# The order of the steps beside the gather slots of a PEER layer, and how many steps stand in each slot

## The chip, the cores and the metric

The kernel runs on one core of a Trainium2 chip. The metric is the device time of one execution in microseconds; before the change three runs gave 883.9, 884.2 and 888.28 us, median 884.2 us. The core has a matrix engine (PE, with its weight loads PEld), a vector engine (DVE), a scalar engine (ACT), a general engine (POOL), which here also issues the gathers, and SyncE (SP), which issues the loads of weights. Each engine runs its instructions in the order in which the program wrote them, so an instruction that waits holds up everything behind it on the same engine. Sixteen DMA engines move the data.

## What is computed

One decoder layer over 256 positions of width 1024, in float32. Two groups of attention heads (MoBA, which is plain causal attention at this length, and differential attention) share one input projection; their output goes through `w_out` and is added to `x`. Then comes PEER, a retrieval of single-neuron experts:

```python
x = x + mixed @ w_out
q  = (xc @ w_query).reshape(C, 8, 2, 128)          # xc: the normed x, 128 tokens a chunk
sc = einsum('thpd,hpnd->thpn', q, sub_keys)
top_s, top_i = top_k(sc, 16)                       # of each half, then of the 256 sums
best_s, best_pos = top_k(cand_s, 16)
u, vv = expert_down[experts], expert_up[experts]   # 8 heads x 16 experts a token
act = gelu(einsum('cd,chkd->chk', xc, u))
out = einsum('chk,chkd->cd', softmax(best_s) * act, vv)
```

Each of the 256 tokens needs 128 experts, and each expert is a row of 2048 floats (down and up side by side): 268.85 MB of gathered rows.

## The kernel before

The tokens are two tiles of 128: A (the first half) and B (the second). A tile goes through six projections (`proj`, then `evac` with norm and RoPE, and `turn` for the transposes), attention by group (`scores`, `probsT`, `attend`, `mixturn`, together `both`), the output product (`wout`), the residual and its transposes (`resid`), the norm (`norm`), and then four **routings**: `route(tt, c4)` computes the queries of two heads (`query`) and picks their experts (`choose`: `keys`, `route1`, `route2`), which makes 32 more of the tile's 128 columns of expert numbers known (`ready` counts them).

A **slot** is one column of experts for the 128 tokens of a tile, 256 slots in all, A's 128 first. Its gather (L604, issued by POOL) brings 128 rows of 8 KB, 1.05 MB, into a buffer of a ring. `dot` (L614, DVE) multiplies the down half with the normed token and sums; `weigh` (L620 to L626, ACT) makes gelu, the gate and a diagonal matrix; `add` multiplies the up half with that diagonal on PE into `acc` (L638), or, in every fourth slot of A, adds it on DVE (L636). In the program's order `add` of a slot comes one slot behind its `dot`, and once `lag` is 1 `weigh` comes a slot later as well. After `add` the buffer is free and `issue()` writes the next gather, as long as expert numbers are known.

The ring starts with 4 buffers (`RING0`). Five more (`RING1`) come when the space of the projections' weights and work tiles is given back, and six more (`RING2`) when the attention's space is.

All of A up to its first half routing, and B's projections 5, 4 and 2, are written ahead of the slots. The rest is cut into **steps** by Python generators and written between the slots, in an order that is fixed by hand (`tc.manual_schedule()`), so the order of each engine's instructions is just the order of this program:

- `front()` is B up to its norm: projections 3, 0 and 1 (15 + 13 + 15 = 43 steps); in the 44th step the ring grows from 4 to 9 and `lag` becomes 1; attention of the two groups (16 steps each); `wout` with its loads (2 loads and 16 pairs of k and n: 18 steps; `wo2` holds 4 tiles of weights, half of what is needed, so the second half of the load waits for the first half of the products); `resid` 3, `norm` 2. Together 98 steps; after the last the ring has 15.
- `route(A, c4)` and `route(B, c4)`: 20 steps each, 8 of `query` and 12 of `choose`. After `query` the next routing's weights are loaded (`load_q`).
- `mix(r, f, nr, nf)` takes nf steps of f after every nr steps of r. `behind()` puts them in their order, and the loop at the end (L744 to L749) writes a slot, then steps until there are `STEPS` = 2 for each slot so far, then the gathers that are possible.

Before the change the order is: the other half of the first routing (12 steps), then route(A, 1) with one step of front after every two (30 steps), route(A, 2) and route(A, 3) with one after every one (40 each), the 48 steps left of front, and then B's four routings.

Weights of B's projections come through 8 tiles (`wts`), four to a projection, so that the load of the second next projection waits for the one whose tiles it takes over; each waits on SP, in the order of the program.

Of the kernel before, what the change touches and what calls it, by code (L numbers as in the profile page):

```python
# [45 lines left out]
RING1 = 5  # L46
RING2 = 6
WRING = 8
STEPS = 2.0

DVE_ADD = 4

# [2 lines left out]
def hymba_peer_kernel(ctx, tc, xT_d, x_d, an_d, fn_d, fnT_d, win_d, qkg_d, lam_d, og_d, wout_d,  # L55
# [324 lines left out]
    A, B = 0, 1  # L380
# [84 lines left out]
    def load_q(c4, pool):  # L465
        W["q", c4] = []
        fetch(("q", c4), wq_d[c4], pool)

    def query(tt, c4, parts=((0, 4),)):
        w = W["q", c4]  # L470
        q = rt1.tile([P, 4, P], FT, name="qs", tag="qs")
        qs[tt, c4] = q
        for a, b in parts:
            p = ps().rearrange("p (a b) -> p a b", b=P)
            for c in range(a, b):
                for k in range(KC):
                    PE.matmul(p[:, c], lhsT=w[k // 2][:, k % 2, c * P:(c + 1) * P], rhs=xgT[tt][:, k],  # L477
                              start=(k == 0), stop=(k == KC - 1))
                    if k % 4 == 3 and (c, k) != (b - 1, KC - 1):
                        yield  # L480
            S.copy(q[:, a:b], p[:, a:b])
            yield

    def keys(tt, c4, a, b):
        sc = scp.tile([P, 4, NKEY], FT, name="sc")[:, :b - a]
        p = ps().rearrange("p (a b) -> p a b", b=NKEY)[:, :b - a]
        for c in range(a, b):
            PE.matmul(p[:, c - a], lhsT=qs[tt, c4][:, c], rhs=sk[:, c4 * 4 + c], start=True, stop=True)
        S.activation(sc, p, AF.Copy, scale=r2[tt])  # L489
        scs[tt, c4, a] = sc  # L490
        yield
# [73 lines left out]
    def route2(tt, c4, h0, nh):  # L565
        hits, g = rs1.pop((tt, c4, h0))
        c0 = (c4 * 2 + h0) * TOPK
        fv = ef[tt][:, c0:c0 + nh * TOPK].rearrange("p (h k) -> p h k", h=nh)
        for i, e in enumerate(hits):
            V.tensor_reduce(fv[:, :, 8 * i:8 * i + 8], e, axis=AX.X, op=OP.add)  # L570
        V.tensor_copy(eid[tt][:, c0:c0 + nh * TOPK], ef[tt][:, c0:c0 + nh * TOPK])
        gz = small.tile([P, 2], FT, name="gz")[:, :nh]
        V.tensor_reduce(gz, g, axis=AX.X, op=OP.add)
        V.reciprocal(gz, gz)
        V.tensor_tensor(g, g, bc(gz, TOPK), op=OP.mult)

    def choose(tt, c4, h0=0, nh=2):
        yield from keys(tt, c4, 2 * h0, 2 * h0 + 2 * nh)
        yield from route1(tt, c4, h0, nh)
        yield  # L580
        route2(tt, c4, h0, nh)
        ready[0] += nh * TOPK

    def route(tt, c4, then=None):
        yield from query(tt, c4)
        if then is not None:
            load_q(then, wqp)
        yield from choose(tt, c4)
# [3 lines left out]
    rows, made, ready, done = {}, [0], [0], [0]  # L592
# [4 lines left out]
    def issue():  # L597
        while made[0] < ready[0] and rings:
            n = made[0]
            made[0] += 1  # L600
            tt, k = n // NSEL, cols[n]
            home[n] = rings.pop(0)
            rows[n] = home[n].tile([P, 2 * D], FT, name="uv")
            G.indirect_dma_start(out=rows[n], out_offset=None, in_=uv_d,  # L604
                                 in_offset=bass.IndirectOffsetOnAxis(ap=eid[tt][:, k:k + 1], axis=0))

    acc, lag, dots, ready_w = {}, [0], [], []
# [40 lines left out]
    def slots(n):  # L648
        for _ in range(n):
            dot()  # L650
            last = done[0] == NT * NSEL
            while len(dots) > (0 if last else lag[0]):
                weigh()
            while len(ready_w) > (0 if last else 1):
                add()
# [31 lines left out]
    def front():  # L687

        for g in (3, 0, 1):
            yield from project(g)  # L690
        pj.close()
        wst.close()
        bs = ExitStack()
        bp["b"] = bs.enter_context(tc.tile_pool(name="bp", bufs=1, side="right"))
        xb = ctx.enter_context(tc.tile_pool(name="xb", bufs=1))
        rings.extend([ctx.enter_context(tc.tile_pool(name="gat1", bufs=RING1))] * RING1)
        lag[0] = 1
        yield from both(B, MOBA)
        yield from both(B, DIFF)
        bs.close()  # L700
        wo2 = right.enter_context(tc.tile_pool(name="wo2", bufs=4, side="right"))
        for q in (0, 2):
            for n in range(2):
                fetch(("o", n, B), wout_d[n], wo2, (q, q + 1))
            yield
            for k in range(2 * q, 2 * q + 4):
                for n in range(2):
                    wout(B, n, k, psB)
                    yield
        yield from resid(B, xb)  # L710
        yield from norm(B, xb)
        right.close()
        rings.extend([ctx.enter_context(tc.tile_pool(name="gat2", bufs=RING2, side="right"))] * RING2)

    def mix(r, f, nr, nf):
        n = 0
        for _ in r:
            yield
            n += 1
            if n % nr == 0:  # L720
                for _ in range(nf):
                    next(f, None)
                    yield

    def behind():
        f = front()
        yield from choose(A, 0, 1, 1)
        yield from mix(route(A, 1, 2), f, 2, 1)
        yield from mix(route(A, 2, 3), f, 1, 1)
        yield from mix(route(A, 3), f, 1, 1)  # L730
        for _ in f:
            yield
        yield from route(B, 3, 2)
        yield from route(B, 2, 1)
        yield from route(B, 1, 0)
        yield from route(B, 0)

    ctx.enter_context(tc.manual_schedule())
    issue()
    work = behind()  # L740
    for _ in range(1):
        next(work)
    steps = 0
    while done[0] < NT * NSEL:  # L744
        slots(1)
        while steps < STEPS * (done[0] + 1):
            next(work, None)
            steps += 1
        issue()  # L749


# [54 lines left out]
```

## Time and profile before

| | |
|---|---|
| runs | 883.9, 884.2, 888.28 us; median 884.2 us |
| the profiled execution | 884.77 us, span 883.0 us from its first to its last instruction |
| moved by DMA in the span | 318.95 MB, 361 GB/s on average |
| of it gathers | 268.85 MB |
| first gather issued, first dot | at 103.7 us, at 112.8 us |
| PE, DVE, POOL, ACT busy | 688.5, 542.2, 411.7, 303.1 us |

The span is cut below at dots: a row with a line's name counts the two instructions of each dot (the product and the read of its sum), so 28 instructions are 14 slots. "PEclk" is the share of the full clock that PE was granted, "DMA share" the mean busy share of the DMA engines, GB/s what they moved. Times are in microseconds from the start of the span.

### The profile page before, as it was taken

What the parts mean: (1) busy time and instruction counts of PE and PEld (TensorE: products, weight loads), DVE (VectorE), ACT (ScalarE), POOL (GpSimd) and SP (SyncE); (2) the same over time, 40 slices, a digit from 0 to 9 for tenths busy, and PEclk for the clock granted to TensorE, in tenths of its full rate; (3) what the DMA queues carried; (4) which work ended last, traced back from release to release, by engine and by line L of the source; (5) the groups of instructions that cost most, each with busy time, mean ns of one, the idle gap of its engine ahead of it and who ended that gap; (6) DMA issues with size and microseconds to landing.
All of it is one profiled execution on the core that took longest, in us unless ns stands there. A gap on an engine that the chain in (4) does not pass through costs nothing.

```text
span 883.0 us, 8001 instructions
## 1 busy us (share of the span) xinstructions
PE 688.5 (78%) x2028; PEld 321.6 (36%) x2028; DVE 542.2 (61%) x1417; ACT 303.1 (34%) x909; POOL 411.7 (47%) x438
## 2 busy tenths in 40 slices
PE   6999959668559686867968769699888777877786
PEld 2555525234225243433625435244222222222222
DVE  4753485684694986671777876994455445554453
ACT  1322143133232363631233332454333333333332
POOL 3310363354362582232564764775555555455540
PEclk9999989899879877978989799799999999999999
DMA  9991779989969889789899999899999999999995
GB/s 352 348 371 42 275 273 341 419 317 351 416 239 321 301 355 403 245 311 379 332 416 418 420 417 419 311 409 419 419 420 419 421 420 419 420 420 421 419 419 212
DMA packets 51534, 318.95 MB, mean 361 GB/s; under 512 B 6112, under 2 KB 6368, under 8 KB 18592
## 3 DMA queue, kind: packets, MB, share of 16 engines
q0 software_dynamic: 36944, 268.85, 76.4%
q1 hardware_dynamic: 14112, 48.93, 14.5%
q10 hardware_dynamic: 432, 0.66, 0.2%
q8 instruction: 17, 0.28, 0.1%
q14 instruction: 29, 0.24, 0.1%
HBM read 317.36 MB, written 1.05 MB: 361 GB/s over the span
## 4 chain that ended last, share of the span: by engine, by line
DMA 44%; PE 25%; DVE 14%; issue 8%; POOL 5%; ACT 3%; POOLq 0%; DVEq 0%; SPq 0%; ACTq 0%
DMA uv<-in_uv_dram,eid 41%; PE acc L638 8%; PE psB L184 6%; DVE uv L614 5%; PE psA L477 3%; PE psB L352 3%; POOL uv L604 3%; DVE x L636 1%; POOL hit L556 1%; DMA w<-in_win_dram 1%; DMA w<-in_wq_dram 1%; DMA w<-in_wout_dram 1%; PE psA L254 1%; PE psA L303 1%; ACT L620 1%
## 5 line engine op out<-in xcount | busy, mean ns | idle before, releaser
L638 PE MATMUL acc<-uv,dg 128*128 128x512 f32 x896 | 464.6, 649 | 151.2 <-ACT dg L626 149.8
L604 POOL DMA_INDIRECT uv<-in_uv_dram,eid x256 | 319.2, 1247 | 352.0 <-PE acc L638 138.2
L614 DVE SCALAR_TENSOR_TENSOR uv<-uv,xn 128x1024 f32<-128x1024 f32 x256 | 314.0, 1237 | 216.7 <-DMA uv<-in_uv_dram,eid 213.4
L638 PEld LDWEIGHTS acc<-uv,dg 128*128 128x128 f32 x896 | 164.1, 200 | 407.8 <-ACT dg L626 269.4
L620 ACT ACTIVATE hdot<-hdot 128x1 f32<-128x1 f32 x256 | 51.3, 200 | 351.1 <-DVE uv L614 350.8
L626 ACT ACTIVATE dg<-ident,hdot 128x128 f32<-128x128 f32 x224 | 89.9, 401 | 42.4 <-PE acc L638 35.8
L184 PE MATMUL psB<-w,xT 128*128 128x512 f32 x192 | 94.9, 631 | 7.2 <-DMA w<-in_win_dram 7.2
L621 ACT ACTIVATE hdot<-hdot,gate 128x1 f32<-128x1 f32 x256 | 75.3, 294 | 8.3
L477 PEld LDWEIGHTS psA<-xgT,w 128*128 128x128 f32 x512 | 65.0, 197 | 19.0 <-issue 18.7
L477 PE MATMUL psA<-xgT,w 128*128 128x128 f32 x512 | 64.7, 279 | 0.0
L184 PEld LDWEIGHTS psB<-w,xT 128*128 128x128 f32 x192 | 37.5, 203 | 50.4 <-issue 48.5
L498 POOL TENSOR_TENSOR ci<-tf 128x4 f32<-128x4 f32 (+5 forms) x81 | 20.9, 291 | 58.8 <-DVE tf L526 58.8
L636 DVE SCALAR_TENSOR_TENSOR x<-uv,hdot,x 128x1024 f32<-128x1024 f32 x32 | 43.7, 1364 | 0.0
L352 PE MATMUL psB<-w,mT 128*128 128x512 f32 x64 | 30.9, 616 | 5.9 <-DMA w<-in_wout_dram 5.9
L556 POOL TENSOR_TENSOR hit<-hit,ci 128x160 f32<-128x160 f32 (+1 forms) x32 | 30.0, 968 | 0.5 <-DVE hit L553 0.4
L214 POOL TENSOR_TENSOR qt<-pr,rS 128x128 f32<-128x128 f32 (+1 forms) x24 | 18.2, 784 | 23.8 <-ACT pr L195 23.8
L510 DVE MAX8 tops<-sc 128x8 f32<-128x128 f32 x32 | 7.1, 280 | 23.4 <-ACT sc L489 23.4
L614 DVE DVE_READ_ACCUMULATOR uv<-uv,xn 128x1 f32 x256 | 20.8, 81 | 0.0
L352 PEld LDWEIGHTS psB<-w,mT 128*128 128x128 f32 x64 | 12.3, 198 | 20.8 <-issue 13.2
L570 DVE TENSOR_REDUCE ef<-hit 128x16 f32<-128x320 f32 (+3 forms) x18 | 11.8, 665 | 9.7 <-POOL hit L556 9.7
L360 DVE TENSOR_TENSOR x<-psB,x 128x512 f32<-128x512 f32 x4 | 2.8, 691 | 24.1 <-PE psB L352 24.1
L620 ACT ACT_TABLE_LOAD x13 | 16.7, 1283 | 0.2
(126 smaller groups left out, 417.7 us busy)
## 6 DMA issues: line engine op xcount, KB each, us to landing
w<-in_win_dram SPq DMA_DIRECT2D x40, 512.0 KB, 8.4
w<-in_wq_dram SPq DMA_DIRECT2D x28, 512.0 KB, 8.6
w<-in_wout_dram SPq DMA_DIRECT2D x16, 512.0 KB, 9.9
uv<-in_uv_dram,eid POOLq DMA_INDIRECT x256
sk<-in_sk_dram SPq DMA_DIRECT2D x1, 1024.0 KB
out_dram<-x SPq DMA_DIRECT2D x4, 256.0 KB, 2.0
xT<-in_xT_dram SPq DMA_DIRECT2D x2, 256.0 KB
x<-in_x_dram ACTq DMA_DIRECT2D x1, 512.0 KB
```

The source lines that it names most:

```text
L184: PE.matmul(p, lhsT=xT[tt][:, k], rhs=W[ci, tt][k // 2][:, k % 2], start=(k == 0), stop=(k == KC - 1))
L352: PE.matmul(wops[tt, n], lhsT=mixT[tt, MOBA if k < 4 else DIFF][:, k % 4], rhs=W["o", n, tt][k // 2][:, k % 2], start=(k == 0), stop=(k == ...
L477: PE.matmul(p[:, c], lhsT=w[k // 2][:, k % 2, c * P:(c + 1) * P], rhs=xgT[tt][:, k], start=(k == 0), stop=(k == KC - 1))
L498: eng.tensor_tensor(d, src[:, :, 1, b0:b0 + nb], src[:, :, 0, a0:a0 + 1].to_broadcast([P, src.shape[1], nb]), op=OP.add)
L556: G.tensor_tensor(e[:, h], e[:, h], ci[:, h, None, :n].to_broadcast([P, 8, n]), op=OP.mult)
L604: G.indirect_dma_start(out=rows[n], out_offset=None, in_=uv_d, in_offset=bass.IndirectOffsetOnAxis(ap=eid[tt][:, k:k + 1], axis=0))
L614: V.scalar_tensor_tensor(uv[:, :D], uv[:, :D], 1.0, xn[n // NSEL], op0=OP.mult, op1=OP.mult, accum_out=h)
L620: S.activation(h, h, AF.Gelu)
L621: S.activation(h, h, AF.Copy, scale=gate[n // NSEL][:, col:col + 1])
L626: S.activation(dg, ident, AF.Copy, scale=h)
L636: V.scalar_tensor_tensor(x2[tt], uv[:, D:], dg, x2[tt], op0=OP.mult, op1=OP.add)
L638: PE.matmul(acc[tt][:, c], lhsT=dg, rhs=uv[:, D + c * 512:D + (c + 1) * 512], start=(k == 0), stop=(k == NSEL - 1))
```

## The change

`STEPS` becomes a table of four rates, and `behind()` sets which of them holds. The half routing that is left is mixed with three steps of front to each of its own, and front then goes on alone until `lag` is set, that is until the projections are done and the ring has nine buffers. All that at four steps a slot. Then route(A, 1) alone at three a slot, route(A, 2) and route(A, 3) with one step of front after each of theirs and then the rest of front at two a slot, and B's routings at 1.2 a slot. The instructions themselves, their number and their data stay as they are.

```diff
-STEPS = 2.0
+STEPS = (4, 3, 2, 1.2)
...
+    rate = [0]
+
     def behind():
         f = front()
-        yield from choose(A, 0, 1, 1)
-        yield from mix(route(A, 1, 2), f, 2, 1)
+        yield from mix(choose(A, 0, 1, 1), f, 1, 3)
+        while not lag[0]:
+            next(f)
+            yield
+        rate[0] = 1
+        yield from route(A, 1, 2)
+        rate[0] = 2
         yield from mix(route(A, 2, 3), f, 1, 1)
         yield from mix(route(A, 3), f, 1, 1)
         for _ in f:
             yield
+        rate[0] = 3
         yield from route(B, 3, 2)
...
-    for _ in range(1):
-        next(work)
+    next(work)
     steps = 0
     while done[0] < NT * NSEL:
         slots(1)
-        while steps < STEPS * (done[0] + 1):
+        steps += STEPS[rate[0]]
+        while steps >= 1:
             next(work, None)
-            steps += 1
+            steps -= 1
         issue()
```

## The prediction

> **What bounds the kernel now.** I read the page's slices first: the span, how busy the DMA engines are, and what they move.
>
> ```profile
> span 883.0 us, 8001 instructions
> ...
> DMA  9991779989969889789899999899999999999995
> GB/s 352 348 371 42 275 273 341 419 317 351 416 239 321 301 355 403 245 311 379 332 416 418 420 417 419 311 409 419 419 420 419 421 420 419 420 420 421 419 419 212
> ```
>
> Forty slices of 22.1 us. From slice 20 on, the core moves some 420 GB/s: there nothing but the DMA engines decides, and one slice from the end shows it in full, beside the one dip:
>
> ```profile
> 551.90:573.90 22.00, 13.17 (x22) 4.93 (x22) 21.27 (x65) 9.07 (x25) 16.10 (x24) 0.77 0.85 311
> 838.90:860.90 22.00, 17.75 (x36) 6.09 (x36) 11.10 (x18) 7.68 (x27) 9.61 (x7) 1.00 1.01 420
> ```
>
> A slot's gather is 1.05 MB, so at 420 GB/s it takes 2.50 us, and no order of steps makes that half faster. What can be won lies before, where the rate falls to 239 or 245. I therefore cut the span where the program changes, at dots 0, 14, 53, 61 and 85 and at the end of B's routing.
>
> ```profile
> core 0: us, PE busy (x) PEld busy (x) DVE busy (x) ACT busy (x) POOL busy (x), PEclk, DMA share, GB/s
> 112.80:164.90 52.10, 36.41 (x124) 19.25 (x125) 35.19 (x114) 16.94 (x46) 23.34 (x30) 0.87 0.84 324
> 164.90:307.20 142.30, 99.32 (x313) 49.69 (x311) 101.01 (x279) 44.21 (x127) 65.68 (x84) 0.90 0.89 330
> 307.20:333.50 26.30, 21.95 (x74) 11.11 (x73) 21.90 (x64) 18.34 (x45) 21.51 (x29) 0.81 0.93 367
> 333.50:399.60 66.10, 46.38 (x167) 25.47 (x168) 44.26 (x97) 27.58 (x81) 16.88 (x16) 0.82 0.84 318
> 399.60:433.90 34.30, 28.41 (x97) 14.88 (x96) 12.70 (x28) 5.25 (x17) 11.26 (x10) 0.90 0.91 349
> 433.90:573.20 139.30, 101.25 (x379) 56.62 (x379) 111.50 (x375) 50.08 (x141) 88.46 (x111) 0.88 0.99 399
> 573.20:883.00 309.80, 249.80 (x518) 89.44 (x516) 159.34 (x261) 113.33 (x384) 158.70 (x116) 1.00 0.98 404
> ```
>
> The same stretches for the dots alone give the number of slots (two instructions a dot):
>
> ```profile
> core 0: us, DVE busy (x), PEclk, DMA share, GB/s
> 112.80:164.90 52.10, 17.59 (x28) 0.87 0.84 324
> 164.90:307.20 142.30, 50.46 (x79) 0.90 0.89 330
> 307.20:333.50 26.30, 9.65 (x15) 0.81 0.93 367
> 333.50:399.60 66.10, 22.74 (x41) 0.82 0.84 318
> 399.60:433.90 34.30, 6.06 (x11) 0.90 0.91 349
> ```
>
> So slots 0 to 13 took 52.1 us (3.72 each), 14 to 52 142.3 us (39 slots, 3.65), 53 to 60 26.3 us (8, 3.29), the next 20.5 took 66.1 (3.22), the last 5.5 of this part 34.3 (6.2). In no stretch before 433.9 is any engine full: PE is at 70% (36.41 of 52.1, 99.32 of 142.3), DVE at 68 and 71%, DMA at 0.84 to 0.89. The work is a ring of waits: a buffer is filled, read, added and only then filled again. With four buffers that ring sets the pace. The fifth comes at 316 us; POOL's timeline shows the gathers no longer waiting for an add:
>
> ```profile
> 309.51 0.94 POOL L604 DMA_INDIRECT uv<-in_uv_dram,eid  x1 [1.47 <-PE acc L638]
> ...
> 316.18 0.94 POOL L604 DMA_INDIRECT uv<-in_uv_dram,eid  x1 [0.30 <-issue]
> ...
> 322.39 1.45 POOL L604 DMA_INDIRECT uv<-in_uv_dram,eid  x1 [0.30 <-issue]
> ```
>
> **The order, counted in steps.** Before: 12 steps of the half routing, 30 of the first mix (10 of them front's), 40 of the second (20 of front's), then front's 44th step stands 28 steps into the third. That is step 110, slot 54 at two a slot. The third mix ends at step 122, front 48 steps later at 170, slot 84; B's routings at 250, slot 124. After: 12 + 36 mixed and 8 more steps of front bring its 44th at step 56, slot 14. Route(A, 1) needs 20 at three: slot 21. Two mixes of 40 at two: slot 61, with 84 of front's steps done. The last 14: slot 68. B's 80 at 1.2: slot 135. Expert numbers suffice throughout: 16 until slot 12, where the ring of four wants 16; 32 until slot 21, where nine buffers want 30; 64 to slot 41. The full ring of 15 comes at slot 68 in place of 84.
>
> **Stage 1, slots 0 to 13, four buffers, four steps.** The costs:
>
> ```profile
> L184 PE MATMUL psB<-w,xT 128*128 128x512 f32 x192 | 94.9, 631 | 7.2 <-DMA w<-in_win_dram 7.2
> ...
> L477 PE MATMUL psA<-xgT,w 128*128 128x128 f32 x512 | 64.7, 279 | 0.0
> ```
>
> A projection's products take 94.9/12 = 7.9 us, a query's 64.7/8 = 8.1. An add takes PE 64.63/29 = 2.2 us a slot (four instructions; a quarter of A's slots have none):
>
> ```profile
> 164.90:307.20 142.30, 64.63 (x116) 22.11 (x116) 0.90 0.89 330
> 307.20:333.50 26.30, 13.11 (x21) 4.45 (x21) 0.81 0.93 367
> 333.50:399.60 66.10, 25.75 (x45) 9.14 (x46) 0.82 0.84 318
> ```
>
> PE has 3 x 7.9 = 23.7 us of projections (8 steps of 0.99 us, three to a slot, ahead of the older slot's add) and 14 x 0.75 x 2.2 = 23: 47 us. DMA has 14 gathers and three projections' weights, 14.7 + 6.3 = 21 MB, 50 us at 420. At this ring's shares, 70% and 0.87, that is 67 and 57 us. I take 64, 4.6 a slot against 3.7 now. The bounds are 50 (DMA full) and 82 (PE's 47 and the 35 of DVE in these slots one after the other): the evacuations' chains (ACT, DVE, POOL, DVE, PE) come closer together, and POOL's part of them stands ahead of the gathers. SP's order changes too: three projections' loads now stand ahead of `load_q`, and they may be late:
>
> ```profile
> w<-in_wq_dram SPq DMA_DIRECT2D x20, 512.0 KB, 12.9
> w<-in_win_dram SPq DMA_DIRECT2D x9, 512.0 KB, 27.6
> ```
>
> The last projection's load starts when the third one's products are done, some 21 steps of front (seven slots, 32 us) before its own products; the median landing of 27.6 us fits in, barely. The next query's load has four slots, some 16 us, for 12.9. These waits stand in the 82.
>
> **Stage 2, slots 14 to 20.** In the stretch of B's routings DVE is busy 111.50 us, of which the dots and adds have these:
>
> ```profile
> L638 PE MATMUL acc<-uv,dg 128*128 128x512 f32 x127 | 72.9, 708 | 35.3 <-ACT dg L626 35.3
> ...
> L614 DVE SCALAR_TENSOR_TENSOR uv<-uv,xn 128x1024 f32<-128x1024 f32 x44 | 53.4, 1238 | 0.1
> ...
> L636 DVE SCALAR_TENSOR_TENSOR x<-uv,hdot,x 128x1024 f32<-128x1024 f32 x11 | 15.5, 1407 | 0.0
> ```
>
> 111.5 - 53.4 - 15.5 - 3.5 (reads of the sums, 44 x 0.08) leaves 39 us for four routings, 9.8 each. Seven slots need 7 x 1.66 + 9.8 = 21 us of DVE; at that stretch's 80% that is 27 us (bounds 21 and 34; the gathers for five more buffers go out here).
>
> **Stage 3, slots 21 to 60: nine buffers, one routing and one attention step a slot.** Slots 53 to 60 of before are just this mix: 3.29 us. The next stretch has two attention steps a slot and no routing: 3.22. By work: attention has 21.95 + 46.38 - 13.11 - 25.75 = 29 us of PE in these two stretches, 7 of it output products; with 40 x 0.75 x 2.2 = 66 of adds and two queries, 16, PE has 111 us; at 83% (21.95 of 26.3) 134, 3.35 a slot. DMA has 42 MB of gathers and 8.4 of weights, 120 us. I take 3.45, 138 us, a little over the rows, as queries (8.1 us each) and attention meet on PE. Bounds 120 and 167 (4.18, the mean from 333.5 to 433.9).
>
> **Stage 4, slots 61 to 67.** The same 14 steps took 34.3 us, and 11 of them were a wait for the second half of `w_out`:
>
> ```profile
> 399.64 10.97 DMA w<-in_wout_dram
> ```
> and from the timeline of DVE:
> ```profile
> 421.30 0.69 DVE L360 TENSOR_TENSOR x<-psB,x 128x512 f32<-128x512 f32 x1 [15.98 <-PE psB L352]
> ```
>
> DVE waited 16 us at that place, with the dots behind it. Now the first half's products stand one to a slot, beside a routing, and the load of the second half starts as each tile comes free; only the last tiles, freed just ahead, can be late. I take 8 of the 11 us off: 26 us; bounds 23 and 34.
>
> **The rest.** From dot 85 (433.9) to the end are 449.1 us. From dot 68 there are 17 gathers more, 42.5 us. The 1.2 steps keep DVE at 1.66 + 1.2 x 9.8/20 = 2.25 us a slot, below 2.50, where two steps gave 2.64; of the dip of 22 x (1 - 311/420) = 5.7 us I take off 3. No new wait is added; tail and B's slots stay.
>
> **The sum:** 112.8 + 64 + 27 + 138 + 26 = 367.8 for dot 68 (slot 84 at 433 before), and 367.8 + 449.1 + 42.5 - 3 = 856.4 us of span. The profiled execution lies 1.8 us over its span (884.77 against 883.0), 0.6 over the median of 884.2: **858 us**.
>
> A rule of the Trainium skill speaks against any gain: DMA: Bandwidth & Descriptors, Where 436 GB/s comes from, has transfers from HBM bound at about 358 GB/s a core. By it the 361 GB/s of the whole span are the limit already, and the sum would stay at 884. The trace disagrees: 420 GB/s in the slice quoted above.
>
> The other rule is for the change. TensorE: Matmul & The Clock Gate, Part 1, says that PE is slowed to half its clock once it has been idle for a window of some 3.4 us. The rows show 0.87 granted in the first stretch and 1.00 in the last one; if denser products kept the clock at 1.00, 47 us of PE would be 41, and the sum an estimated 6 us less. I leave this out.
>
> **The rivals.**
> - *The DMA engines are full from slot 21 on.* Nine buffers are enough and stage 3 takes its 120 us: 858 - 18 = 840. For it speaks 0.93 of DMA share from 307.2 to 333.5; against it 0.84 in the next stretch with the same buffers.
> - *The steps' time is only moved.* Buffers weren't the limit, the steps' chains were, and they cost what they did: 321.1 us from dot 0 to dot 85, less 17 slots at 2.5 us, puts dot 68 at 391.4, 23.6 later than the sum: 882. For it speaks that nine buffers gave 3.22 to 4.18 a slot, hardly below four buffers' 3.65.
> - *Adds come late on PE, and it is slower.* With nine buffers POOL still waited for PE's adds:
>
> ```profile
> POOL uv L604 <- PE acc L638: 56.3, 15, 9.4
> ```
>
>  In stage 3 an add stands behind a query's products and attention's transposes, and those wait for DVE. If every slot pays this, at 4.18 us, stage 3 is 167 us (+29) and stage 4 stays at 34 (+8): 895. It decides from 4.2 us a slot on alone: (888.6 - 858)/40 = 0.77 over 3.45. Against it speak the 3.29 of the very mix.
> - *The whole span's 361 GB/s is what the core can draw, whatever the order:* then DMA is the bound everywhere and the time stays at 884. Twenty slices at some 420 speak against it. This is the first of the two rules above.
>
> **Chances.** Forecast 0.58, full DMA 0.14, moved time 0.15, late adds 0.12, capped rate 0.01. A difference of 0.5%, 4.4 us, is about what a measurement tells from none: faster is below 879.8, slower above 888.6. So faster 0.72, same 0.16, slower 0.12. The forecast's own case runs from 840 (stage 1 at 57, stage 3 at 127) to 876 (stage 1 at 74, stage 3 at 146). The range takes in the moved time and stops short of the late adds: 840 to 890.
>
> **What would show it.** POOL's burst of five gathers stands near 177 us instead of 316; dot 21 near 204, dot 61 near 342, dot 68 near 368 (+-15). DMA is over 0.93 from dot 14 on and full from dot 68; the dip near 560 is gone. The wait for `w_out` shrinks from 11 us to a few. Wrong would be: stage 1 over 82 us with POOL waiting for adds or PE for weights, stage 3 over 4 us a slot, or a DMA rate below 400 after dot 68.

## The result and the profile after

The changed kernel took 848.25, 848.48 and 852.76 us, median 848.48 us against 884.2 us: a ratio of 0.960, 95% interval 0.954 to 0.966. Measured once more, beside the experiments below, it had 0.963 (0.960 to 0.966). The forecast was 858 us, with a range from 840 to 890.

These are the span, the DMA engines' share and their rate in the forty slices of the changed kernel; a slice is 21.2 us now. Lines of the code are one higher than before (L605 is the gather, L615 the dot, L639 the add on PE).

```profile
span 846.5 us, 8001 instructions
...
DMA  9992798669899999999999999999999999999993
GB/s 350 352 356 91 244 409 332 230 263 406 302 395 376 369 409 382 420 417 419 420 418 420 417 419 420 421 420 420 420 418 421 420 421 418 420 421 420 420 419 155
```

The full rate of 420 GB/s begins at slice 16, 339 us, in place of slice 20, 442 us, and it has no dip after that before the last slice. The lowest slices that are left are 3 and 4, ahead of the first dot (111.7 us), and 7 and 8, in stage 1 and at its end.

The same cut as in the prediction, at dots 0, 14, 21, 61 and 68 of the changed kernel (columns as before):

```profile
core 0: us, PE busy (x) PEld busy (x) DVE busy (x) ACT busy (x) POOL busy (x), PEclk, DMA share, GB/s
111.70:177.50 65.80, 45.17 (x98) 18.99 (x96) 49.57 (x135) 20.22 (x52) 31.93 (x43) 0.88 0.77 295
177.50:214.60 37.10, 28.31 (x123) 19.91 (x124) 22.08 (x87) 10.12 (x26) 21.49 (x28) 0.78 0.92 369
214.60:333.30 118.70, 103.44 (x416) 60.02 (x414) 99.59 (x290) 59.17 (x169) 62.87 (x72) 0.92 0.97 374
333.30:356.80 23.50, 21.33 (x69) 11.31 (x70) 16.00 (x33) 6.53 (x21) 8.06 (x8) 0.93 1.01 420
356.80:846.50 489.70, 376.25 (x958) 158.27 (x956) 291.43 (x672) 176.12 (x569) 259.70 (x245) 0.96 0.99 408
```

| stage of the changed kernel | forecast, us | measured, us | short of 420 GB/s, us |
|---|---|---|---|
| start to dot 0 | 112.8 | 111.7 | |
| 1: slots 0 to 13 | 64 | 65.8 | 65.8 x (1 - 295/420) = 19.6 |
| 2: slots 14 to 20 | 27 | 37.1 | 4.5 |
| 3: slots 21 to 60 | 138 | 118.7 | 13.0 |
| 4: slots 61 to 67 | 26 | 23.5 | 0 |
| the rest | 488.6 | 489.7 | 14.0 |

The last column says where the time came from: it is the time in which the bytes that were not moved would have been moved. Both kernels move the same bytes (318.95 and 318.93 MB), so this sum has to come out; it shows in which stretch the time was won, and the cause has to come from the runs below. The same sum over the seven stretches of the kernel before, from its rows in the prediction, is 11.9 + 30.5 + 3.3 + 16.1 + 5.8 + 7.0 + 11.8 = 86.4 us; now it is 51.1. The 35.3 us between them and the 1.1 us by which dot 0 came sooner are, but for rounding, the 36.5 us between the two spans. Stage 1 costs 7.7 us more than before; all else is gain, and nearly all of it lies between dots 14 and 85.

In a second profile of the changed kernel the five stretches from dot 0 took 64.2, 36.9, 124.6, 18.0 and 493.6 us. The border between stages 3 and 4 thus moves by some 6 us from one execution to another, while the two together take the same time (142.2 and 142.6 us).

POOL's timeline shows the five new buffers being filled, at the place that was forecast (177 us, 316 before):

```profile
176.96 1.42 POOL L605 DMA_INDIRECT uv<-in_uv_dram,eid  x1
178.69 1.95 POOL L605 DMA_INDIRECT uv<-in_uv_dram,eid  x1 [0.30 <-issue]
...
185.96 0.94 POOL L605 DMA_INDIRECT uv<-in_uv_dram,eid  x1 [0.30 <-issue]
```

### The profile page after: what moved, and what is told of

Same layout as the page of the kernel before. It is cut to its first block, busy times and chain, and to the rows that moved or that the text cites. A ratio compares the mean times of both kernels' runs of the same rounds, so it can differ in the third digit from the quotient of the medians.

```text
span 846.5 us, 8001 instructions
## 1 busy us (share of the span) xinstructions
PE 679.3 (80%) x2028; PEld 323.8 (38%) x2028; DVE 535.0 (63%) x1417; ACT 299.9 (35%) x907; POOL 410.4 (48%) x438
## 2 busy tenths in 40 slices
DMA packets 51534, 318.93 MB, mean 377 GB/s; under 512 B 6113, under 2 KB 6369, under 8 KB 18593
## 4 chain that ended last, share of the span: by engine, by line
DMA 43%; PE 31%; DVE 16%; issue 4%; ACT 3%; POOL 2%; DVEq 0%; POOLq 0%; SPq 0%; ACTq 0%
DMA uv<-in_uv_dram,eid 41%; PE acc L639 10%; PE psB L185 7%; PE psA L478 5%; DVE uv L615 5%; PE psB L353 3%; PE psA L255 1%; DMA w<-in_win_dram 1%; DVE x L637 1%; PE psA L489 1%; DMA w<-in_wout_dram 1%; DVE topi L514 1%; POOL uv L605 1%; DVE topi L523 1%; DVE s L517 1%
## 5 line engine op out<-in xcount | busy, mean ns | idle before, releaser
L639 PE MATMUL acc<-uv,dg 128*128 128x512 f32 x896 | 455.3, 639 | 129.2 <-ACT dg L627 123.5
L605 POOL DMA_INDIRECT uv<-in_uv_dram,eid x256 | 316.7, 1237 | 312.4 <-DMA uv<-in_uv_dram,eid 141.6
L615 DVE SCALAR_TENSOR_TENSOR uv<-uv,xn 128x1024 f32<-128x1024 f32 x256 | 311.1, 1227 | 163.7 <-DMA uv<-in_uv_dram,eid 161.2
L639 PEld LDWEIGHTS acc<-uv,dg 128*128 128x128 f32 x896 | 163.8, 199 | 379.2 <-ACT dg L627 233.6
L627 ACT ACTIVATE dg<-ident,hdot 128x128 f32<-128x128 f32 x224 | 89.9, 401 | 21.2 <-PE acc L639 14.4
L185 PE MATMUL psB<-w,xT 128*128 128x512 f32 x192 | 89.8, 617 | 6.9 <-DMA w<-in_win_dram 6.9
L478 PEld LDWEIGHTS psA<-xgT,w 128*128 128x128 f32 x512 | 69.4, 207 | 21.3 <-issue 20.3
L478 PE MATMUL psA<-xgT,w 128*128 128x128 f32 x512 | 69.3, 289 | 0.0
L185 PEld LDWEIGHTS psB<-w,xT 128*128 128x128 f32 x192 | 37.2, 199 | 51.1 <-issue 49.1
L499 POOL TENSOR_TENSOR ci<-tf 128x4 f32<-128x4 f32 (+5 forms) x81 | 27.8, 375 | 55.6 <-DVE tf L527 55.5
L557 POOL TENSOR_TENSOR hit<-hit,ci 128x160 f32<-128x160 f32 (+1 forms) x32 | 27.0, 873 | 2.9 <-DVE hit L554 2.5
L215 POOL TENSOR_TENSOR qt<-pr,rS 128x128 f32<-128x128 f32 (+1 forms) x24 | 15.6, 675 | 24.1 <-ACT pr L196 24.0
L615 DVE DVE_READ_ACCUMULATOR uv<-uv,xn 128x1 f32 x256 | 20.9, 82 | 0.0
L196 ACT ACTIVATE pr<-psB,r 128x512 f32<-128x512 f32 x8 | 5.5, 685 | 36.8 <-PE psB L185 31.2
L482 ACT COPY qs<-psA 128x512 f32<-128x512 f32 (+1 forms) x9 | 4.8, 536 | 36.6 <-PE psA L478 36.6
## 6 DMA issues: line engine op xcount, KB each, us to landing
w<-in_wq_dram SPq DMA_DIRECT2D x28, 512.0 KB, 11.8
```

What stands on the lines that cost most here:

```text
L185: PE.matmul(p, lhsT=xT[tt][:, k], rhs=W[ci, tt][k // 2][:, k % 2], start=(k == 0), stop=(k == KC - 1))
L499: eng.tensor_tensor(d, src[:, :, 1, b0:b0 + nb], src[:, :, 0, a0:a0 + 1].to_broadcast([P, src.shape[1], nb]), op=OP.add)
L557: G.tensor_tensor(e[:, h], e[:, h], ci[:, h, None, :n].to_broadcast([P, 8, n]), op=OP.mult)
L615: V.scalar_tensor_tensor(uv[:, :D], uv[:, :D], 1.0, xn[n // NSEL], op0=OP.mult, op1=OP.mult, accum_out=h)
L627: S.activation(dg, ident, AF.Copy, scale=h)
L639: PE.matmul(acc[tt][:, c], lhsT=dg, rhs=uv[:, D + c * 512:D + (c + 1) * 512], start=(k == 0), stop=(k == NSEL - 1))
```

## The experiments

Two theories were set against each other. *Buffers*: nine buffers from slot 14 keep DMA fed while attention runs. *Order*: one attention step beside one routing step a slot hides the chains (work that passes from engine to engine, each waiting for the one before), whatever the ring. A third question was the slow end (1.2 steps a slot), a fourth the second routing alone. Ratios are to the kernel before, run beside it on the same chip, with 95% intervals.

| run | what differs | ratio | interval |
|---|---|---|---|
| changed kernel | | 0.960; again 0.963 | 0.954 to 0.966; 0.960 to 0.966 |
| late_buffers | 4 buffers to slot 54, lag from slot 54 | 1.002 | 0.999 to 1.005 |
| four_lag | 4 buffers to slot 54, lag from slot 14 | 1.011 | 1.008 to 1.014 |
| lag_late | 9 buffers from slot 14, lag from slot 54 | 0.981 | 0.977 to 0.984 |
| two_of_five | 6 buffers from slot 14, 9 from 54, lag from 14 | 0.973 | 0.968 to 0.977 |
| before_lag | the kernel before, lag from slot 0 | 1.022 | 1.019 to 1.025 |
| before_slow_end | the kernel before, B's routings at 1.2 | 0.995 | 0.993 to 0.998 |
| rate_2_end; rate_2_again | B's routings at 2 | 0.959; 0.968 | 0.955 to 0.963; 0.965 to 0.971 |
| second_mixed | second routing with front's steps | 0.972 | 0.970 to 0.975 |
| query_early | its query beside the projections | 0.962 | 0.959 to 0.965 |
| six_first | six steps a slot in stage 1 | 0.962 | 0.958 to 0.965 |

**The new buffers and the lag kept back.** The order of all steps is the changed one; only what the 44th step of front hands out waits for slot 54.

```diff
-        rings.extend([ctx.enter_context(tc.tile_pool(name="gat1", bufs=RING1))] * RING1)
-        lag[0] = 1
+        g1 = ctx.enter_context(tc.tile_pool(name="gat1", bufs=RING1))
+        rings.extend([g1] * 0)
+        late.extend([g1] * 5)
+        opened[0] = 1
...
+    opened, late = [0], []
...
-        while not lag[0]:
+        while not opened[0]:
...
+        if done[0] == 54:
+            rings.extend(late)
+            lag[0] = 1
         slots(1)
```

> The changed order of steps with the five more buffers, and the lag of one, kept back until slot 54, where the kernel before had them. Theory 'buffers': four buffers set the pace (3.65 us a slot in the kernel before), so slots 14 to 53, now with attention beside them, go from 134 us to 142 to 156, and the time is 858 to 875 us. Theory 'order': what counts is one attention step beside one routing step a slot, and buffers do not; then the time stays within 4 us of 848.

888.42 us, the time of the kernel before. The order by itself, all of it, is worth nothing; "order" fell, and "buffers" was right in the sign but too small in the size, since it had priced four buffers at 10 to 27 us and they, with the lag that came late, cost some 36 (from 0.960 or 0.963 to 1.002 of 886). The window of slots 21 to 52 shows it, first of the changed kernel, then of this one:

```profile
214.60:311.90 97.30, 82.69 (x369) 51.15 (x368) 80.55 (x226) 49.78 (x144) 46.69 (x47) 0.90 0.97 375
```
```profile
217.70:342.00 124.30, 89.78 (x369) 54.12 (x368) 82.55 (x226) 51.40 (x144) 41.35 (x47) 0.84 0.81 296
```

The same number of instructions on every engine (369 on PE, 226 on DVE), 97.3 us against 124.3, and 375 GB/s against 296. DVE's work is nearly the same too, 80.55 and 82.55 us.

**Two buffers of the five.** `[g1] * 2` at slot 14 and `[g1] * 3` at slot 54, with the lag at slot 14.

> The changed kernel with two of the five more buffers at slot 14 (a ring of six) and three at slot 54. Theory 'buffers': between 848 and the time of the run with four buffers, and nearer to 848, as each further buffer covers less. Theory 'order': 848 within 4 us.

0.973, so two of the buffers give some three quarters of the way from four_lag (below, 1.011) to the changed kernel. The same window:

```profile
213.40:317.30 103.90, 84.48 (x369) 51.12 (x368) 82.20 (x226) 49.87 (x144) 47.87 (x47) 0.89 0.91 354
```

**All five buffers, the lag later.** As late_buffers, but all five buffers go into the ring at slot 14.

> The changed kernel with all five buffers at slot 14, but the lag of one between dot and weigh set only at slot 54. Theory 'buffers': within 4 us of 848, since the lag only helps where the scalar engine is late. Rival 'lag': the scalar engine stands between a dot and its add, and without the lag the adds and with them the gathers come later: 855 or more.

0.981: the rival was right, the lag alone is worth 1.8 to 2.1% here. The window again, then who waited for whom from 214 to 335 us (engine, line and tile that waited, what for; us in total, times, longest), of this run and of the changed kernel. The changed kernel does more in these 121 us, 42 dots against 34:

```profile
216.50:332.50 116.00, 86.22 (x367) 52.73 (x366) 81.65 (x227) 50.77 (x144) 42.20 (x46) 0.84 0.84 317
```
```profile
ACT hdot L621 <- DVE uv L615: 45.0, 17, 7.3
...
PE psA L342 <- DVE ao L335: 17.8, 2, 10.1
DVE mx L260 <- PE psA L255: 13.7, 3, 8.3
```
```profile
ACT hdot L621 <- DVE uv L615: 18.3, 14, 4.6
...
PE psA L342 <- DVE ao L335: 10.1, 2, 5.4
...
DVE mx L260 <- PE psA L255: 2.5, 2, 1.6
```

Without the lag `weigh` of a slot stands in ACT's order right behind its dot, so ACT waits for DVE 45.0 us in place of 18.3, and what it does for attention comes later: DVE then waits for PE's scores 13.7 us in place of 2.5, and PE for `attend` 17.8 in place of 10.1. By these waits it is the attention's chain that the lag frees. That ACT's place is what passes it on is argued from them and wasn't tried by itself.

**The lag without the buffers,** once in the changed order (`[g1] * 0` and `lag[0] = 1` at slot 14) and once in the kernel before:

```diff
-    acc, lag, dots, ready_w = {}, [0], [], []
+    acc, lag, dots, ready_w = {}, [1], [], []
```

> The changed kernel with the five more buffers kept back until slot 54, but the lag of one from slot 14 on. Theory 'both': buffers alone took 1.002 to 0.980 and the lag then 0.980 to 0.960; if the two add, the lag alone gives some 0.98. Theory 'one needs the other': a lag holds two more buffers, and of four only two are then ahead, so it gives nothing or costs: 1.00 or more.

> The kernel before with a lag of one from the first slot, nothing else: the part of the change that could be had without its order. Theory 'both' (lag helps by itself): 0.98 of the kernel before. Theory 'one needs the other': 1.00 or more, since the ring has four buffers until slot 54 there.

1.011 and 1.022: with four buffers the lag costs. Slots 21 to 52 of the first one:

```profile
218.30:351.80 133.50, 94.49 (x373) 56.27 (x372) 82.37 (x227) 51.19 (x144) 45.24 (x48) 0.81 0.76 284
```

So the lag needs the buffers, and the buffers give half as much without it. The rates in this window are 284 GB/s with four buffers and the lag, 296 with four and none, 317 with nine and none, 354 with six and the lag, 375 with nine and the lag. DVE's waits for gathers from 217 to 345 us, with four buffers and the lag (four_lag), then with four and none (late_buffers):

```profile
DVE uv L615 <- DMA uv<-in_uv_dram,eid: 46.3, 20, 6.2
```
```profile
DVE uv L615 <- DMA uv<-in_uv_dram,eid: 24.9, 14, 4.6
```

By the program's order a lag holds a buffer for a slot longer, and of four that leaves one fewer to be filled ahead; with it DVE waits 46.3 us for data in place of 24.9.

**The slow end.** `STEPS = (4, 3, 2, 2)`, measured twice, the second time beside the changed kernel, and the kernel before with 1.2 steps a slot in B's routings and nothing else:

```diff
+        slow[0] = 1
         yield from route(B, 3, 2)
...
-    steps = 0
+    owed = [2.0]
...
-        while steps < STEPS * (done[0] + 1):
+        owed[0] += 1.2 if slow[0] else STEPS
+        while owed[0] >= 1:
             next(work, None)
-            steps += 1
+            owed[0] -= 1
```

> The changed kernel with B's routings at 2 steps a slot in place of 1.2. Theory 'slow end' (3 us in the forecast's sum): vector work rises from 2.25 to 2.64 us a slot, the ring runs full of undone slots and DMA dips as it did near 560 us before: 851 to 854. Rival: 15 buffers and the light slots of B absorb it: 847 to 850.

> The changed kernel with B's routings at 2 steps a slot, beside the changed kernel on the same chip. Theory 'slow end': 3 to 6 us over the changed kernel. Rival: within 2 us of it; the first look gave 0.959 of the kernel before, as the changed kernel had.

> The kernel before with one part of the change alone: B's routings at 1.2 steps a slot. Theory 'slow end': the dip near 560 us goes, and the time falls by 3 to 6 us, to 878 to 881. Rival: nothing, 883 to 886, as the ring's slack moves the same loss elsewhere.

In the kernel before it is 0.995, some 4 us, clear of its interval. In the changed one it is not settled: 852.66 us the first time, 0.959 and no different; 857.65 us against 852.98 the second time, 4.7 us more, with intervals that overlap by a little. The dip itself did return; two slices of rate_2_again, in which the changed kernel has 418 and 420 GB/s:

```profile
485.40:506.80 21.40, 13.58 (x25) 5.48 (x26) 19.86 (x60) 10.04 (x29) 16.57 (x23) 0.84 0.88 333
506.80:528.10 21.30, 19.97 (x45) 7.70 (x44) 21.30 (x33) 11.82 (x41) 17.34 (x14) 1.00 1.00 407
```

DVE has 41.16 of the 42.7 us there, and 21.4 x (1 - 333/420) + 21.3 x (1 - 407/420) = 5.1 us of DMA are lost.

**The second routing alone.** Stage 2 is where the sum was most too low, 37.1 for 27 us. DVE's timeline of it:

```profile
184.76 0.08 DVE L615 DVE_READ_ACCUMULATOR uv<-uv,xn 128x1 f32 x1
195.33 0.87 DVE L511 MAX8 tops<-sc 128x8 f32<-128x128 f32 x4 [10.49 <-ACT sc L490]
```

Between two dots DVE stood 10.5 us for the keys' scores, which need the whole query first: the vector engine has nothing else in its order there. In the wait itself DMA moved 417 GB/s:

```profile
184.84:195.33 10.49, 9.81 (x65) 8.19 (x64) 0.01 (x1) 1.30 (x3) 2.69 (x3) 0.94 1.01 417
```

In the stretch that lent the forecast its 80% (the kernel before, 433.9 to 573.2 us) the same wait was 19.4 us for four routings, under 5 each on average:

```profile
DVE tops L510 <- ACT sc L489: 19.4, 4, 6.7
```

A rival is PE's clock. From 177.5 to 184.8 us the granted clock was 0.50, right behind 5.4 us in which PE had waited for DVE, and the query's 64 products kept PE busy for 9.9 us. But in six_first (below) they took 7.4 us at 0.99, and DVE still waited 11.2 us, so the clock is not what makes this wait.

Two attempts to fill the wait, the first with front's steps, the second by laying the query beside the projections:

```diff
-        yield from route(A, 1, 2)
+        yield from mix(route(A, 1, 2), f, 2, 1)
```

> The changed kernel with the second routing not alone: one step of front after every two of its own, still three steps a slot (30 steps, ten slots). Theory 'query alone': stage 2 took 37 us in place of 27 because the vector engine waited 10.5 us for the query's products; mixed, that wait shrinks below 5 us. DMA had 369 GB/s there, so at most 37 x (1 - 369/420) = 4.5 us can come back: 844 to 848. Rival: the wait only moves to the next query, and expert numbers come three slots later: 848 to 853.

0.972, slower than the changed kernel, and the wait stayed (12.4 us; the row above it is POOL waiting for buffers):

```profile
POOL uv L605 <- PE acc L639: 18.4, 4, 8.3
DVE tops L511 <- ACT sc L490: 12.4, 1, 12.4
```

"Query alone" fell in this form. In the order of this run front's attention steps stand ahead of parts of the query on PE; that they hold it up and give DVE nothing that is ready is argued from this order, not shown. That expert numbers come at slot 24 in place of 21, where nine buffers want 33 and 32 are known, may have its share; it wasn't taken apart.

```diff
-        yield from mix(choose(A, 0, 1, 1), f, 1, 3)
+        yield from mix(choose(A, 0, 1, 1), f, 1, 2)
+        r = route(A, 1, 2)
+        n = 0
         while not lag[0]:
             next(f)
             yield
+            n += 1
+            if n > 4 and n % 2 == 0:
+                next(r)
+                yield
         rate[0] = 1
-        yield from route(A, 1, 2)
+        yield from r
```

> The changed kernel with the second routing's query laid beside the last steps of the projections (two steps of front beside each step of the half routing, then one query step after every two of front), the rest of that routing alone behind it. Theory 'query alone': its products fill PE's idle third in stage 1 and the wait of 10.5 us at the vector engine goes: 842 to 848. Rival 'stage 1 is PE's': the eight steps more make stage 1 longer by their 8 us and DMA, at 295 GB/s there, loses what stage 2 gains: 848 to 854.

The wait shrank to 7.6 us and nothing came of it, 0.962 against 0.963. Seven of the query's eight steps stand ahead of front's 44th here, so that the new buffers come at slot 16 in place of 14, and their gathers are issued until 193 us in place of 186; the run doesn't tell the gain of the one from the loss of the other.

```profile
DVE tops L511 <- ACT sc L490: 7.6, 1, 7.6
```

Stage 2 of the changed kernel moves 369 GB/s as a whole, and 417 while DVE waits, since the nine buffers are being filled: its 10 us over the forecast cost 4.5 us of DMA at most, and hardly any of that in the wait.

**Six steps a slot in stage 1,** `STEPS = (6, 3, 2, 1.2)`, tried as a version that might beat the changed kernel.

> The changed kernel with six steps a slot in place of four until the projections are done: nine buffers and the lag from slot 9 on instead of 14. Stage 1 is the one stretch that still moves only 295 GB/s. Theory 'steps set stage 1': its 56 steps take some 55 us in place of 66 whatever the number of slots beside them, and 2 to 5 us come back, some 0.958 of the kernel before. Rival 'slots and buffers set it': the slots' adds come later behind more steps, DMA falls further, and the time is that of the changed kernel or more, 0.963 to 0.97.

0.962, the same. The first row is slots 0 to 8, the second slots 9 to 13, and the third the first 5 us of the second:

```profile
112.30:167.40 55.10, 38.01 (x83) 16.42 (x82) 40.83 (x123) 17.42 (x40) 27.47 (x38) 0.85 0.72 280
167.40:192.40 25.00, 20.86 (x110) 14.26 (x110) 13.78 (x65) 6.53 (x17) 10.14 (x20) 0.92 0.73 283
```
```profile
167.40:172.40 5.00, 4.76 (x13) 2.42 (x15) 4.72 (x8) 0.98 (x3) 0.00 (x1) 0.61 0.01 3
```

The steps of the projections took some 55 us as expected, but at 280 GB/s, and then DMA stood still: until 167.4 us DVE was held by the last projection, with dots behind it in its order; POOL issued no gather between 160.42 and 172.40 us, and the new buffers were filled from there on. The changed kernel has the same seam at the end of its stage 1: no gather between 169.59 and 176.96 us, and 122 GB/s from 170 to 180. Six steps bring it 5 us earlier and don't shorten it. No version tried beats the changed kernel beyond its interval.

## Why the prediction held, and where it missed

- **The bound.** Right: DMA decides once it is fed, and what was won is time in which it had not been. From dot 68 to the end the forecast had 488.6 us and 489.7 were measured.
- **The order in slots.** Right: nine buffers at slot 14 (177 us), dot 61 at 333.3 (342 forecast), dot 68 at 356.8 (368). The DMA share was 0.92 in stage 2, just under the 0.93 that was named, and above it in the others from there on.
- **Stage 1.** 65.8 for 64 us. 4.7 us a slot at 295 GB/s against 3.7 at 324: the price of four steps beside four buffers was foreseen. The seam at its end, some 7 us of DMA from 170 to 180 us, had no term of its own.
- **Stage 2, "that stretch's 80%".** The failed step of the sum: 37.1 for 27 us. DVE's 22.08 us of work had been priced at 21; what was left out is that a routing written alone makes DVE wait for its own query, 10.5 us, where the stretch that lent the 80% has under 5 us a routing on average, with 15 buffers and its dots at hand. Why it is shorter there wasn't tried.
- **Stage 3, "I take 3.45".** The term that was mis-sized the other way: 2.97 us a slot, 118.7 us for 138. PE was busy 103.44 us, not 111, and for 87% of the time, not 83. The time is near that of the rival "full DMA" (120, with 0.14 of the chance), but not for its reason: DMA moved 374 GB/s, 13.0 us short of full, and only 44.44 MB where 50.4 had been counted. Stage 2, longer than forecast, had moved 13.7 MB where seven gathers are 7.3, so that the +10 of the one and the -19 of the other are in part one error. The lag had no price of its own; it was in the row of 3.29 us without being named. lag_late shows that without it 19 us come back (116.0 in place of 97.3 in slots 21 to 52). One row was also misread: from dot 61 to dot 80 are 19 slots, not 20.5, so the 66.1 us are 3.48 a slot and not 3.22, and the 3.45 lay between the rows and not over them.
- **Stage 4.** 23.5 for 26 us. The wait for `w_out` shrank from 11 us to 7.8, not to a few. It stands mostly at the end of stage 3, and DMA moved 426 GB/s from 327.5 to 335.3 us, so it costs DMA nothing:

```profile
327.54 7.79 DMA w<-in_wout_dram
```

- **The slow end** was put at 3 us; 4 in the kernel before, 0 to 5 here.
- **"The steps' time is only moved"** (0.15) had 882, and late_buffers gave 888: as a time it would have been right for the order without the buffers. Its reason, that buffers weren't the limit, fell with the same run. "Late adds" did not come about: 2.97 us a slot against its 4.2.
- **The pages.** The trace goes on against the Trainium skill, DMA: Bandwidth & Descriptors, Where 436 GB/s comes from: 420 GB/s from 339 us on, where its bound from HBM would be about 358. That section gets the 358 by dividing the 716 GB/s of a memory stack between two cores, and this kernel runs on one. The estimate from TensorE: Matmul & The Clock Gate, Part 1, of the Trainium skill did not come true in stage 1: the granted clock was 0.88 there, as before (0.87).

The two errors of +10 and -19 us are most of the 10 us between forecast and result. As far as they are not one error (stage 3 above), it is luck that they had opposite signs.

## What to carry to other kernels

Where a ring of buffers feeds a DMA that could be kept full, see whether what frees space for more buffers can come first, even if the stretch until then gets slower: here it cost 7.7 us and gave 43, together with the lag and the slow end. A deeper software pipeline (the lag) and more buffers are one decision: the lag cost 1 to 2% with four buffers and gave 2% with nine, as much as the nine buffers gave without it. Judge a stall by the bytes that were not moved in it, not by its length: the 10 us in which the vector engine waited in stage 2 went by at 417 GB/s.

## What was not expected of the hardware

The DMA share isn't the rate: from 214.6 to 333.3 us it was 0.97 at 374 GB/s, where 1.01 stands for 420. And spans differ by some 4 us before the edit matters: dot 0 came at 111.7 us in the changed kernel and at 115.9 in four_lag, whose steps up to there are the same, so that a difference of single microseconds is to be read from several runs and not from one profile's span.
